# Turning v, p and three quarters of x2 with VectorE's block transpose through DRAM instead of TensorE, in a hybrid RWKV-7 and pooling trunk

## The chip, the cores and the metric

The kernel runs on one core of a Trainium2 chip. The metric is device time in microseconds (us) of the whole program, a median over several runs; a profiled execution has a time of its own, which is always told apart from the median here. The engines are named as in the profile: PE is TensorE's matmul, PEld its weight load, DVE is VectorE, ACT is ScalarE, POOL is GpSimd, SP is the sync engine, which here only issues DMAs. SPq and ACTq are the DMA issues of SP and of ACT.

## The reference

One layer of a decoder trunk on `x` of 512 positions by 2048 features, all float32: an input projection, 16 RWKV-7 heads of 64 beside a pooling branch, an output projection with a residual, and a gated embedding.

```python
h = rms_norm(x, norm_g)
z = h @ w_in                       # r, k, v, decay and rate inputs | gate | pool input | pool gate
zs = zs + (token_shift(zs) - zs) * mu
decay = exp(-exp(-softplus(-(w0 + tanh(wd) @ w_up)) - 0.5))
a = sigmoid(a0 + ad @ a_up)
kk = (k * k_k).reshape(B, T, N_HEADS, HEAD_SIZE)
kk = kk / maximum(norm(kk, axis=-1, keepdims=True), KK_EPS)
k = k * (1 + (a - 1) * k_a)
# per head and position: S = S (diag(w) - kk^T (a kk)) + v^T k;  y = S r
y = head_group_norm(wkv7_scan(r, decay, k, v, kk, a), ln_w, ln_b)
y_rwkv = (y + sum(r * k * r_k) * v) * silu(gate)
y_pool = per_group_matmul(windowed_mean(u) - u, w_pool) * pool_scale * silu(pool_gate)
x = x + concat(y_rwkv, y_pool) @ w_out
gate = sigmoid(x @ w_pg + b_pg)
x = x + gate * (p @ w_ple)
return rms_norm(x, final_g)
```

## The kernel before

Each large matrix product is made of three products of 128x128 by 128x512 blocks: an operand is split into a high part, which is a rounded copy (`whi`, `hhi`, `yhi`, `x2hi`: an ACT cast), and the rest (`wlo` and so on: a DVE subtraction). `wsplit` (L126 to L134) does that for a weight block: a DMA on SP into `raw`, the ACT cast at L132, the DVE subtraction at L133. The pools `raw`, `whi` and `wlo` hold four blocks each.

The program has three stretches. **The first** (to 715 us) makes h, transposes it, and then runs the input projection as a stream of matmuls: `pump(n)` (L492) puts the next n steps of that stream (the column groups z of k, r, v and the gate of each pair of heads, and the pooling units `zb`, `pp` and `pple`) into PE's program between the small matmuls of the recurrence, so that PE's order is fixed and the recurrence's waits are covered by the stream. The recurrence goes through eight groups j, each of two heads. For each of them:

- `prepare(j)` makes from k, r, v the scaled operands `ar` (L594, L597), `bk` (L596), `kp`, and stores `bk` to DRAM (`bkd`), from where it is read back turned in blocks of 32 by 32 (`bg`, L662).
- `invert(j)` is a substitution of 31 steps of two small DVE operations (L674, L678) on `xw`, with the rows `n` that were stored to `nd` and loaded back spread over the partitions. Its steps are interleaved with the eight chunks of `recur(j-1)`: `step` lets HN = 2 of them follow each hop after the HS-th, ordered behind the DVE product `zs` of that hop. Its result goes to DRAM (`xd`) and back into `x1`, by four stores and four loads on SP.
- `gather(j)` computes decay and rate of group j+1 (`pu`, `pa` with the small weights `ur`, `ar` and their splits `us`, `as`, L526), turns v (`pv`, four transposes on PE, with two ACT copies at L707 and L708 into `uv`), sums the squares of k per head for group j+1 (`pss`, two matmuls in `norm_key`), turns `x1` (`y1`, two DVE transposes of 32x256 at L732), and then runs the small matmuls `pq`, `pmv` and `px` that finish the inverse.
- the key norm of group j+1 is `max(pss, 1e-24)` (L568) and a reciprocal of the full 128x512 tile (L572) on DVE, in `scale_key`.
- `recur(j)` runs eight chunks, each with PE products `py`, `pu`, `ps`, DVE products `zs` and `sbd`, and ACT copies `uv`. At its end the group's y is normalised (`st`, `mvr`, `rs`, `nt`, `ysb`: L862 to L873), gated (`yo`) and stored to `yd`.

**The second** (715.6 to 895.5 us) multiplies by w_out in `proj`: four groups `ec` of 512 columns, each with 16 steps of k, each step with four accumulators of three matmuls (`acc_o`). After a group `ec` the result is added to x (L1026), stored (`x2d`), and turned for the next stretch: 16 PE transposes (`px`, L1033) with four ACT casts into `x2hi` and four DVE subtractions into `x2lo`.

**The third** (to the end) multiplies by w_pg in the same way (`acc_g`), with the x2 just turned as the moving operand, gates the embedding and normalises.

What sets the order: PE's by the program text with `pump`; on DVE and ACT a scheduler places each instruction by priority and readiness, and `tc.issue_after(a)` forbids an instruction to stand ahead of `a` on its engine; SP issues its DMAs one after another in its own order, and waits where a DMA's source isn't ready or its target isn't free.

## Time and profile before

| | before |
|---|---|
| median of 3 runs | 1085.27 us (1084.38 to 1087.19) |
| profiled execution, time | 1082.7 us |
| its span | 1081.0 us |
| PE busy | 1056.6 us (98%), 5996 instructions |
| DVE busy | 714.0 us (66%), 1851 instructions |
| ACT busy | 441.5 us (41%), 901 instructions |
| granted PE clock | 0.998 of full speed |

The span runs from the first to the last instruction; the profiled execution's time is 1.7 us longer. Busy time of PE counts a matmul from its start to its modelled end, and neighbouring matmuls overlap; what a matmul takes of PE's time is therefore read from the distance between the starts of two matmuls, not from its own duration. The instruction counts are those of the profile.

### The profile page before, as it was taken

To read this page: it belongs to the slowest core of one execution; us is meant where nothing else is said; L and a number is where in the kernel's file an instruction comes from. 1 tells how busy PE (TensorE), PEld (TensorE's weight loads), DVE (VectorE), ACT (ScalarE), POOL (GpSimd) and SP (SyncE) were. 2 spreads that over 40 slices of the span, in tenths; PEclk is the share of its full clock that TensorE was granted. 3 is DMA by queue.
4 is the path that set the end of the run, shared out by engine and by line. 5 is a ranking of instruction groups with operands and counts; after the bars stand their busy time and mean duration, and the time that the engine had idled before them with its cause. 6 is when DMAs were issued, how large, how long until landed. Compare 5 with 4: busy or idle time off the path is not lost.

```text
span 1081.0 us, 17106 instructions
## 1 busy us (share of the span) xinstructions
PE 1056.6 (98%) x5996; PEld 872.1 (81%) x5996; DVE 714.0 (66%) x1851; ACT 441.5 (41%) x901; POOL 75.0 (7%) x180
## 2 busy tenths in 40 slices
PE   5999999999999999999999999999999999999996
PEld 4888878888888887878788788888888888888885
DVE  6676978888779789787887857563432424445356
ACT  7633435335335354353352344553222222333337
POOL 2100010110110100200101201000000000000000
PEclk9999999999999999999999999999999999999999
DMA  7434443342634533434435343774434428355434
GB/s 236 117 115 111 139 116 88 116 120 74 168 88 114 144 89 105 120 89 112 106 91 158 100 129 111 239 243 141 171 121 143 166 98 271 122 182 161 169 98 156
DMA packets 212916, 146.94 MB, mean 136 GB/s; under 512 B 68085, under 2 KB 173150, under 8 KB 212830
## 3 DMA queue, kind: packets, MB, share of 16 engines
q1 hardware_dynamic: 192126, 112.28, 35.9%
q10 hardware_dynamic: 20704, 33.56, 9.4%
q8 instruction: 47, 0.77, 0.3%
q14 instruction: 39, 0.32, 0.1%
HBM read 122.21 MB, written 23.07 MB: 134 GB/s over the span
## 4 chain that ended last, share of the span: by engine, by line
PE 91%; DVE 4%; DMA 3%; ACT 2%; issue 1%; ACTq 0%; SPq 0%; DVEq 0%
PE acc_o L157 16%; PE acc_g L157 16%; PE zb L157 14%; PE zv L157 8%; PE zg L157 8%; PE zr L157 8%; PE zk L157 7%; PE py L157 2%; PE pu L157 2%; PE pple L157 2%; PE pm L157 1%; DMA n<-nd 1%; PE pp L157 1%; PE ps L157 1%; DMA xt<-in_x_dram 1%; PE pmv L157 1%
## 5 line engine op out<-in xcount | busy, mean ns | idle before, releaser
L133 DVE TENSOR_TENSOR wlo_g<-raw_g,whi_g 128x512 fp32r<-128x512 f32 x84 | 57.0, 685 | 74.4 <-ACT whi_g L132 72.3
L157 PE MATMUL zb<-hhi,whi_b 128*128 128x512 f32 x256 | 106.0, 414 | 0.0
L133 DVE TENSOR_TENSOR wlo_o<-raw_o,whi_o 128x512 fp32r<-128x512 f32 x64 | 43.9, 690 | 90.9 <-ACT whi_o L132 90.8
L157 PE MATMUL zb<-hhi,wlo_b 128*128 128x512 f32 x256 | 100.4, 392 | 0.0
L157 PE MATMUL acc_o<-whi_o,ylo 128*128 128x512 f32 x256 | 100.2, 391 | 0.0
L157 PE MATMUL acc_o<-whi_o,yhi 128*128 128x512 f32 x256 | 99.9, 390 | 0.0
L157 PE MATMUL zb<-hlo,whi_b 128*128 128x512 f32 x256 | 99.8, 390 | 0.0
L157 PE MATMUL acc_o<-wlo_o,yhi 128*128 128x512 f32 x256 | 99.7, 389 | 0.0
L132 ACT CAST whi_g<-raw_g 128x512 fp32r<-128x512 f32 x84 | 52.0, 621 | 105.3 <-PE acc_g L157 58.9
L157 PE MATMUL acc_g<-whi_g,x2hi 128*128 128x512 f32 x208 | 81.2, 391 | 0.0
L832 POOL TENSOR_SCALAR s0p<-sbd,pw 64x64 f32<-64x64 f32 x96 | 58.0, 604 | 332.0 <-DVE sbd L825 243.5
L157 PE MATMUL acc_g<-wlo_g,x2hi 128*128 128x512 f32 x208 | 80.9, 389 | 0.0
L157 PE MATMUL acc_g<-whi_g,x2lo 128*128 128x512 f32 x208 | 80.6, 389 | 0.0
L132 ACT CAST whi_o<-raw_o 128x512 fp32r<-128x512 f32 x64 | 39.9, 623 | 96.3 <-PE acc_o L157 96.3
L132 ACT CAST whi_b<-raw_b 128x512 fp32r<-128x512 f32 x64 | 39.7, 621 | 86.7 <-PE zb L157 29.2
L133 DVE TENSOR_TENSOR wlo_b<-raw_b,whi_b 128x512 fp32r<-128x512 f32 x64 | 43.6, 683 | 27.3 <-ACT whi_b L132 27.1
L157 PEld LDWEIGHTS zb<-hhi,wlo_b 128*128 128x128 f32 x256 | 48.0, 188 | 10.9
L678 DVE TENSOR_TENSOR xw<-xw,tm 128x60 f32<-128x60 f32 (+24 forms) x248 | 52.1, 210 | 7.0
L157 PEld LDWEIGHTS acc_o<-wlo_o,yhi 128*128 128x128 f32 x256 | 48.1, 188 | 9.9
L157 PEld LDWEIGHTS acc_o<-whi_o,ylo 128*128 128x128 f32 x256 | 48.1, 188 | 9.8
L157 PEld LDWEIGHTS acc_o<-whi_o,yhi 128*128 128x128 f32 x256 | 48.1, 188 | 9.7
L157 PEld LDWEIGHTS zb<-hhi,whi_b 128*128 128x128 f32 x256 | 48.2, 188 | 8.3
(283 smaller groups left out, 2529.6 us busy)
## 6 DMA issues: line engine op xcount, KB each, us to landing
raw_b<-in_w_in_dram SPq DMA_DIRECT2D x64, 256.0 KB
raw_o<-in_w_out_dram SPq DMA_DIRECT2D x64, 256.0 KB
raw_g<-in_w_pg_dram SPq DMA_DIRECT2D x64, 256.0 KB
raw_k<-in_w_in_dram SPq DMA_DIRECT2D x32, 256.0 KB
raw_r<-in_w_in_dram SPq DMA_DIRECT2D x32, 256.0 KB
raw_v<-in_w_in_dram SPq DMA_DIRECT2D x32, 256.0 KB
raw_g<-in_w_in_dram SPq DMA_DIRECT2D x32, 256.0 KB
bkd<-bk SPq DMA_DIRECT2D x8, 512.0 KB
```

Of the source, the lines that this page charges most:

```text
L132: nc.scalar.copy(hi, raw)
L133: nc.vector.tensor_tensor(lo, raw, hi.bitcast(F32), ALU.subtract)
L157: i = nc.tensor.matmul(*a, **k)
L678: nc.vector.tensor_tensor(xw[:, 0:n_, s + 1:32], xw[:, 0:n_, s + 1:32], tm[:, 0:n_, 0:w_], ALU.add)
L832: nc.gpsimd.tensor_scalar(s0p[hc, :], nxt[hc, hc], pcn[hc], None, ALU.mult)
```

## The change

1. **x2.** `x2d` is laid out by blocks, and for the first three groups `ec` the 16 PE transposes are replaced: during the next group, from step 5 on, SP issues up to three gathers per step (16 in all, `x2g`, each 32 partitions by 16 blocks by 32 elements), and in steps 8, 9, 11 and 12 one DVE transpose each of 128x512 makes `x2t`, which is split as before. The fourth group's turn stays on PE and moves ahead of a step's matmuls.
2. **v.** For the groups after the first, v is stored to `vd`, gathered back by four DMAs of SP (`vg`), and turned by two DVE transposes of 64x512 straight into `uv`. The four PE transposes and the two ACT copies of each such group go.
3. **p.** Eight gathers on SP read p by blocks, and two DVE transposes take the place of eight PE transposes.
4. **Key norm.** For groups 2 to 7 the squares' sum is copied by ACT, two of its rows are stored to DRAM, loaded as 128x8, clamped and inverted by DVE at that size, stored, and loaded twice with a broadcast to 64 partitions, all by SP. Squaring and summing move from `gather` into chunks 4 and 5 of the recurrence of two groups before.
5. **Substitution.** It starts one hop later (HS from 5 to 6) and does one more step at hop 21.
6. **Small weights and stores.** `ur` and `ar` (32 loads) are issued by SP, after the loads of `n`, instead of ACT; their ACT copies are ordered behind a copy of chunk 6 of the recurrence before. Seven stores of `yo` and six of `sgp` move from ACT's queue to SP's.

```diff
     def load_ab(j):
...
-                nc.scalar.dma_start(out=raw[64 * h:64 * h + 64, :], in_=src[0, :, jc])
+                nc.sync.dma_start(out=raw[64 * h:64 * h + 64, :], in_=src[0, :, jc])
...
             if kind == "p":
-                    pt = psM.tile([P, T], F32, name=f"ppt{k}", tag="m")
-                    for tt in range(NT):
-                        tr(pt[:, tt * P:(tt + 1) * P], pn[0][:, tt, k * P:(k + 1) * P], ident)
+                    pt = rw.tile([P, T], F32, name=f"ppt{k}", tag=("kk", "kp")[k])
+                    nc.vector.transpose(pt.rearrange("p (b k) -> p b k", k=32), pn[0][:, k])
...
     def norm_key(j):
...
-        late[0] = nc.vector.tensor_scalar(kk, ps, 1e-24, None, ALU.max)
+        if j < 2:
+            late[0] = nc.vector.tensor_scalar(kk, ps, 1e-24, None, ALU.max)
+            return
+        nc.scalar.copy(kk, ps)
+        nrd = dram.tile([2, T], F32, name=f"nrd{j}", tag="nrd")
+        nc.sync.dma_start(out=nrd, in_=kk[0::64, :])
+        nr = rw.tile([P, 8], F32, name=f"nr{j}", tag="nr")
+        nc.sync.dma_start(out=nr, in_=nrd.rearrange("h (p e) -> (h p) e", e=8))
+        nrs[j] = nr
+
+    def spread_norm(j):
+        nr, kk = nrs.pop(j), kks[j][0]
+        nc.vector.tensor_scalar(nr, nr, 1e-24, None, ALU.max)
+        nc.vector.reciprocal(nr, nr)
+        ird = dram.tile([2, T], F32, name=f"ird{j}", tag="ird")
+        nc.sync.dma_start(out=ird.rearrange("h (p e) -> (h p) e", e=8), in_=nr)
+        for h in range(2):
+            nc.sync.dma_start(out=kk[64 * h:64 * h + 64], in_=ird[h:h + 1].to_broadcast([64, T]))
 
     def scale_key(j):
-        nc.vector.reciprocal(kk, kk)
+        if j < 2:
+            nc.vector.reciprocal(kk, kk)
...
     def prepare(j):
+        if j:
+            vd = dram.tile([P, T], F32, name=f"vd{j}", tag="vd")
+            with tc.issue_after(read[-1].ins):
+                nc.sync.dma_start(out=vd, in_=v_)
+            vgs[j] = rw.tile([P, NT, 4, 32], F32, name=f"vg{j}", tag="t", bufs=4), vd
...
     def scores(j):
+        if j:
+            vg, vd = vgs[j]
+            with tc.issue_after(n_.ins):
+                for q in range(4):
+                    nc.sync.dma_start(out=vg[32 * q:32 * q + 32],
+                                      in_=vd.rearrange("(b k) (c q i) -> q k c b i", b=4, q=4, i=32)[q])
...
     def gather(j):
-            prepare_key(j + 1)
+            if j == 0:
+                prepare_key(1)
...
-        ps = psY.tile([P, T], F32, name=f"pv{j}", tag="y")
-        for tt in range(NT):
-            tr(ps[:, tt * P:(tt + 1) * P], v_[:, tt * P:(tt + 1) * P], ident)
-        pv = ps.rearrange("p (t c) -> p t c", c=P)
-        nc.scalar.copy(uv[0:64, 0::2, :], pv[0:64])
-        nc.scalar.copy(uv[64:128, 1::2, :], pv[64:128])
+        if j:
+            vg, _ = vgs.pop(j)
+            for h in range(2):
+                hr = slice(64 * h, 64 * h + 64)
+                nc.vector.transpose(uv[hr, h::2, :].rearrange("p c (b k) -> p c b k", k=32), vg[hr])
+        else:
...
         with tc.issue_after(yt[0].ins), tc.issue_after(yt[1].ins):
-            end = normed.pop()() if normed else yt[1]
-        if j + 1 < NJ:
-            with tc.issue_after(yt[0].ins), tc.issue_after(end.ins):
+            if normed:
+                normed.pop()()
+            if j + 1 < NJ:
                 scale_key(j + 1)
...
-                    for _ in range(HN):
+                    for _ in range(HN + (hop[0] == HE1)):
                         next(work, None)
...
+            if j + 2 < NJ and ch == 5:
+                norm_key(j + 2)
...
+            if j + 2 < NJ and ch == 4:
+                prepare_key(j + 2)
...
-    HS, HN = 5, 2
+    HS, HN, HE1 = 6, 2, 21
...
-    x2d = dram.tile([T, D], F32, name="x2d", bufs=1)
+    x2d = dram.tile([D // EC, EC // P, T, P], F32, name="x2d", bufs=1)
...
+    RD0, RDN, TURNS = 5, 3, (8, 9, 11, 12)
...
-            nc.scalar.dma_start(out=x2d[rows, es], in_=t_)
+            nc.scalar.dma_start(out=x2d[ec, :, rows, :].rearrange("c t e -> t c e"),
+                                in_=t_.rearrange("p (c e) -> p c e", e=P))
...
+        def turner(blocks, turned, ec=ec):
+            parts = [(c, q) for c in range(EC // P) for q in range(4)]
+
+            def side(i):
+                with tc.issue_after(wmade[0].ins), tc.issue_after(wmade[1].ins), tc.issue_after(wmade[2].ins):
+                    if i >= RD0:
+                        for c, q in parts[:RDN]:
+                            nc.sync.dma_start(out=blocks[32 * q:32 * q + 32, c],
+                                              in_=x2d[ec, c].rearrange("(b k) (q i) -> q k b i", k=32, i=32)[q])
+                        del parts[:RDN]
+                    if i in TURNS:
+                        c = TURNS.index(i)
+                        t_ = turned(c)
+                        nc.vector.transpose(t_.rearrange("p (b k) -> p b k", k=32), blocks[:, c])
+                        split(x2hi[:, 4 * ec + c, :], x2lo[:, 4 * ec + c, :], t_)
...
         if ec < D // EC - 1:
-            turn()
+            side = turner(...)
```

**DVE, before `pq` of group 3.** These are DVE's last twelve instructions up to the second transpose of `x1` into `y1` (`y_...<-x_...`, on which `pq` waits), before the change. `sig`, `kp` and `tha` belong to the decay, key and rate of group 4, `ve`, `rs` and `nt` to the norm of group 2's y.

```order
L591 TENSOR_SCALAR kp_4535<-tha_4311,dprm 128x512
L133 TENSOR_TENSOR wlo_wp_0_2314<-raw_wp_0_2311,whi_wp_0_2313 128x256
L150 TENSOR_TENSOR nt_4272<-nt_4272,rs_4269 128x8
L592 TENSOR_TENSOR kp_4535<-kp_4535,sk_3911 128x512
L151 SCALAR_TENSOR_TENSOR rs_4269<-nt_4272,rs_4269 128x8
L593 TENSOR_SCALAR tha_4311<-tha_4311 128x512
L149 TENSOR_TENSOR nt_4272<-rs_4269,ve_4270 128x8
L568 TENSOR_SCALAR kk_4284<-pss_4342 128x512
L150 TENSOR_TENSOR nt_4272<-nt_4272,rs_4269 128x8
L732 STREAM_TRANSPOSE y_4397<-x_4167 32x256
L151 SCALAR_TENSOR_TENSOR rs_4269<-nt_4272,rs_4269 128x8
L732 STREAM_TRANSPOSE y_4397<-x_4167 32x256
```

And the same place after the change, again the last twelve up to the second transpose.

```order
L615 TENSOR_TENSOR ar_4558<-sr_4101,pw_4340 128x4x2x64
L153 TENSOR_TENSOR nt_4315<-nt_4315,rs_4312 128x8
L133 TENSOR_TENSOR wlo_g_0_2321<-raw_g_0_2318,whi_g_0_2320 128x512
L154 SCALAR_TENSOR_TENSOR rs_4312<-nt_4315,rs_4312 128x8
L777 STREAM_TRANSPOSE y_4431<-x_4234 32x256
L152 TENSOR_TENSOR nt_4315<-rs_4312,ve_4313 128x8
L617 TENSOR_TENSOR bk_4559<-kp_4560,ipw_4341 128x4x2x64
L153 TENSOR_TENSOR nt_4315<-nt_4315,rs_4312 128x8
L618 SCALAR_TENSOR_TENSOR ar_4558<-sk_3936,dprm,pw_4340 128x4x128
L133 TENSOR_TENSOR wlo_g_1_2418<-raw_g_1_2415,whi_g_1_2417 128x512
L154 SCALAR_TENSOR_TENSOR rs_4312<-nt_4315,rs_4312 128x8
L777 STREAM_TRANSPOSE y_4431<-x_4234 32x256
```

The clamp of the key norm (L568) is gone from this place; both products into `ar`, that into `bk` and two weight splits `wlo_g` now stand ahead of the second transpose.

**SP, in the w_out stretch.** Before, the loads of w_out's blocks (`raw_o`) follow each other across the end of a group `ec`.

```order
L129 DMA raw_o_14_8374<-in_w_out_dram 128x512
L129 DMA raw_o_15_8392<-in_w_out_dram 128x512
L129 DMA raw_o_8_8458<-in_w_out_dram 128x512
L129 DMA raw_o_9_8476<-in_w_out_dram 128x512
L129 DMA raw_o_10_8494<-in_w_out_dram 128x512
```

After it, the gathers of the group `ec` that has just ended stand between the loads of the next one (its blocks come in the order 8 to 13, 0 to 7, 14, 15, so `raw_o_1` is the eighth).

```order
L129 DMA raw_o_0_8610<-in_w_out_dram 128x512
L129 DMA raw_o_1_8631<-in_w_out_dram 128x512
L1094 DMA x2g_8494<-x2d 32x16x32 x9
L129 DMA raw_o_2_8652<-in_w_out_dram 128x512
L1094 DMA x2g_8494<-x2d 32x16x32 x3
L129 DMA raw_o_3_8677<-in_w_out_dram 128x512
L1094 DMA x2g_8494<-x2d 32x16x32 x3
L129 DMA raw_o_4_8702<-in_w_out_dram 128x512
L1094 DMA x2g_8494<-x2d 32x16x32
L129 DMA raw_o_5_8721<-in_w_out_dram 128x512
```

Nine gathers now stand between the eighth and the ninth load, and seven more up to the twelfth.

**PE, at the turn of v in group 3.** Before, `pu` and `pa` (the last of `pa` stands first here) are followed by the four transposes and the stream, and the squares' sum `pss` comes three steps later.

```order
L157 MATMUL pa_4308<-lal,uaz_571 128x512
L161 MATMUL pv_4314<-ident,sv_3355 128x128 x4
L157 MATMUL zb_4229<-hhi,whi_b_0_2224 128x512
L157 MATMUL zb_4229<-hlo,whi_b_0_2224 128x512
L157 MATMUL zb_4229<-hhi,wlo_b_0_2225 128x512
L157 MATMUL zb_4229<-hhi,whi_b_1_2230 128x512
L157 MATMUL zb_4229<-hlo,whi_b_1_2230 128x512
L157 MATMUL zb_4229<-hhi,wlo_b_1_2231 128x512
L157 MATMUL zb_4229<-hhi,whi_b_1_2230 128x512
L157 MATMUL zb_4229<-hlo,whi_b_1_2230 128x512
L157 MATMUL zb_4229<-hhi,wlo_b_1_2231 128x512
L157 MATMUL pss_4342<-kqh_4286,blk 128x512
```

After it the stream follows `pa` at once.

```order
L160 MATMUL pa_4345<-lal,uaz_571 128x512
L160 MATMUL zb_4272<-hhi,whi_b_0_2232 128x512
L160 MATMUL zb_4272<-hlo,whi_b_0_2232 128x512
L160 MATMUL zb_4272<-hhi,wlo_b_0_2233 128x512
L160 MATMUL zb_4272<-hhi,whi_b_1_2238 128x512
L160 MATMUL zb_4272<-hlo,whi_b_1_2238 128x512
L160 MATMUL zb_4272<-hhi,wlo_b_1_2239 128x512
```

Between `pa` and `pq` PE has six matmuls fewer. Over the program PE has 84 fewer: the transposes `pv` go from 32 to 4, `px` of x2 from 64 to 16, and those of p from 8 to none.

More of the change, by code (lines that the diff above doesn't have):

```diff
@@ L513, in need @@
         return zt[nm, j]
-    pws, kks, late = {}, {}, [None]
+    pws, kks, nrs, vgs, read, late = {}, {}, {}, {}, [], [None]
     H1, H2, H3, H4, H5, HE = 6, 12, 20, 8, 13, 40
+    tail = []
     def decay_and_rate(j):
@@ L523, in decay_and_rate @@
                                     (ar_, as_, uaz[1], slice(0, 64), slice(64, 128))):
-            nc.scalar.copy(st, raw)
-            nc.scalar.copy(z_[hi, :], raw[hi, :])
+            with tc.issue_after(tail[0].ins) if tail else ExitStack():
+                nc.scalar.copy(st, raw)
+                nc.scalar.copy(z_[hi, :], raw[hi, :])
             nc.vector.tensor_tensor(st[lo, :], raw[lo, :], st[lo, :].bitcast(F32), ALU.subtract)
@@ L716, in gather @@
         d.update(uv=uv)
-        if j + 1 < NJ:
-            norm_key(j + 1)
+        if j == 0:
+            norm_key(1)
+        if 0 < j < NJ - 1:
+            with tc.issue_after(read[-1].ins):
+                spread_norm(j + 1)
         pump(H5)
@@ L892, in gate_out @@
                 nc.vector.tensor_tensor(yo, yo, sg, ALU.mult)
-                nc.scalar.dma_start(out=yd[j], in_=yo)
+                (nc.sync if j + 1 < NJ else nc.scalar).dma_start(out=yd[j], in_=yo)
             return gate_out
@@ L997, in proj @@
                     continue
-            for tt in tts if keep is None or i >= LATE else tts[:-1]:
-                ts_ = slice(tt * P, (tt + 1) * P)
-                first = i == (LATE if keep is not None and tt == NT - 1 else 0)
-                e_ = mm3(acc[tt], hi_[:, k, ts_], lo_[:, k, ts_], wh[:, 0, :], wl[:, 0, :], first, i == KT - 1)
             if aside is not None and i == 2:
@@ L1006, in proj @@
                     recall(0, lp)
-        return acc
+            if side is not None:
+                side(i)
+            for tt in tts if keep is None or i >= LATE else tts[:-1]:
+                ts_ = slice(tt * P, (tt + 1) * P)
+                first = i == (LATE if keep is not None and tt == NT - 1 else 0)
+                e_ = mm3(acc[tt], hi_[:, k, ts_], lo_[:, k, ts_], wh[:, 0, :], wl[:, 0, :], first, i == KT - 1)
+        return acc
+    RD0, RDN, TURNS = 5, 3, (8, 9, 11, 12)
+    side = None
     ples = {}
@@ L1019, in trunk_kernel @@
         es = slice(ec * EC, (ec + 1) * EC)
-        acc = proj(w_out, yhi, ylo, ec, "o", order)
+        acc = proj(w_out, yhi, ylo, ec, "o", order, side=side)
         x2 = []
```

46 lines of the change are left out of this document (31 added, 15 removed).

## The prediction

> **What bounds the kernel now.** I read the page's busy line and chain first, then the stretches, then what PE waited for.
>
> ```profile
> span 1081.0 us, 17106 instructions
> PE 1056.6 (98%) x5996; PEld 872.1 (81%) x5996; DVE 714.0 (66%) x1851; ACT 441.5 (41%) x901; POOL 75.0 (7%) x180
> PE 91%; DVE 4%; DMA 3%; ACT 2%; issue 1%; ACTq 0%; SPq 0%; DVEq 0%
> ```
>
> PE is busy 98% of the span and carries 91% of the chain that ends last. The table by stretch (two parts of the recurrence, w_out; busy time of PE, PEld, DVE, ACT, POOL, then clock, DMA share, GB/s) says that this holds everywhere, and that DVE is the next engine only in the recurrence.
>
> ```profile
> 45.00:330.00 285.00, 284.56 (x1743) 234.38 (x1742) 227.28 (x637) 119.81 (x252) 25.22 (x45) 1.00 0.43 115
> 330.00:640.00 310.00, 306.37 (x2053) 251.05 (x2053) 251.88 (x754) 127.94 (x277) 34.08 (x58) 1.00 0.42 111
> 715.60:895.50 179.90, 179.90 (x818) 148.87 (x817) 68.30 (x104) 52.39 (x88) 0.00 (x0) 1.00 0.43 147
> ```
>
> PE's waits from 45 us on are few; these are the ones inside the recurrence (total, times, longest):
>
> ```profile
> PE py L157 <- DVE sbd L825: 1.4, 2, 0.9
> PE pu L157 <- DVE zs L799: 1.0, 2, 0.6
> PE pbo L157 <- DVE kpl L138: 0.3, 1, 0.3
> ```
>
> So the time is the sum of PE's program plus about 3 us of stalls. Work taken from PE is won in full, unless what replaces it makes PE wait at a place where it now doesn't. The sum is made for PE: removed matmuls, stalls that go, stalls that come.
>
> **x2: 48 transposes off PE.** The chain through w_out, first group and last end:
>
> ```profile
> 715.63 43.52 PE acc_o L157 x192
> 759.15 1.06 PE px L1033 x9
> 895.49 4.53 PE acc_g L157 x20
> ```
>
> One matmul takes 43.52/192 = 0.2267 us; 768 of them are 174.1 us; the stretch lasts 895.49 - 715.63 = 179.86, so three turns cost 5.8 us. The timeline of one turn agrees: nine transposes take 759.98 - 758.99 = 0.99, three and four more 0.24 and 0.35, and after each break the next matmul is some 0.09 longer, 1.84 together.
>
> ```profile
> 758.99 1.23 PE L1033 MATMUL px<-ident,x 128*128 128x128 f32 x9
> 759.98 0.47 PE L157 MATMUL acc_o<-whi_o,yhi 128*128 128x512 f32 x1
> ```
>
> Three times 1.84 is 5.5, which I take: **-5.5 us** (at most -5.8).
>
> **v and p: 36 transposes off PE.**
>
> ```profile
> 327.78 0.60 PE L161 MATMUL pv<-ident,sv 128*128 128x128 f32 x4
> 328.45 0.39 PE L157 MATMUL zb<-hlo,whi_b 128*128 128x512 f32 x1
> 650.78 1.04 PE L161 MATMUL ppt<-ident,pn 128*128 128x128 f32 x8
> 651.66 0.39 PE L157 MATMUL py<-sbd,ar 128*128 128x128 f32 x2
> ```
>
> From the first `pv` to the second stream matmul behind it are 0.67 us, of which one matmul is 0.23: 0.44 per group, seven groups, **-3.1 us**. For p, 651.66 - 650.78: **-0.9 us**. The squares' sum `pss` only moves: nothing. PE's program is 9.5 us shorter.
>
> **What DVE gets.** Its price counts only where PE waits for it.
>
> ```profile
> L572 DVE RECIPROCAL kk<-kk 128x512 f32<-128x512 f32 x8 | 26.7, 3338 | 0.0
> 320.29 0.70 DVE L617 STREAM_TRANSPOSE bkn<-bg 128x512 f32<-128x512 f32 x1
> 320.92 0.13 DVE L678 TENSOR_TENSOR xw<-xw,tm 128x8 f32<-128x8 f32 x1
> 320.97 0.69 DVE L617 STREAM_TRANSPOSE bkn<-bg 128x512 f32<-128x512 f32 x1
> ```
>
> For groups 2 to 7 the reciprocal (3.34 us) and the clamp (0.69, row below) go, two small ones of 128x8 come (0.13 each, like the `xw` row); the two 64x512 transposes of v take 0.63 each, as a 128x512 one does to the start of what follows it (320.29 to 320.92). That is 3.34 + 0.69 - 0.26 - 1.26 = 2.5 us less per group, in a recurrence where DVE's products hold PE up now and then, as here:
>
> ```profile
> 429.90 0.49 PE L157 MATMUL pu<-zs,x 128*128 128x128 f32 x2 [0.61 <-DVE zs L799]
> ```
>
> I count this one and the `pbo` stall as gone: **-0.9 us** (bounds: none, and all 2.7 us of the three rows). The norm now comes by DRAM through two round trips. What needs it is `bk`, and behind that PE's `pm`:
>
> ```profile
> 345.73 0.68 DVE L600 TENSOR_TENSOR bk<-kk,ipw 128x512 f32<-128x512 f32 x1
> 350.70 2.06 PE L157 MATMUL pm<-ar,bk 64*128 64x128 f32 x32
> ```
>
> There are 4.3 us from the end of the one to the start of the other, and the reciprocal's 3.3 us ahead of it go: **0**. If the broadcast came later than that cover, each us beyond it would cost one in each of six groups.
>
> In w_out, DVE is busy 68 of 180 us and receives twelve transposes, 7.6 us: hidden. The substitution ends a hop later: its last `xw` operation, at 320.92 in group 3, goes to about 323, and two round trips of 2.9 us bring `x1` back by 329, before its turn at 332.76 (below): nothing. `ur` and `ar` are loaded behind `n`, most of a recurrence before `pu` needs them, and 14 ACT copies fewer matter nowhere with ACT at 41%: nothing.
>
> **What becomes late: `pq`.** PE's `pq` waits for the second DVE turn of `x1`. In group 3, before:
>
> ```profile
> 325.50 1.34 DVE L862 BATCH_NORM_STATS2 st<-ysb 128x6 f32<-128x64 f32 x8
> 327.30 0.66 DVE L138 TENSOR_TENSOR kql<-kk,kqh 128x512 fp32r<-128x512 f32 x1
> 332.09 0.69 DVE L568 TENSOR_SCALAR kk<-pss 128x512 f32<-128x512 f32 x1
> 333.27 0.43 DVE L732 STREAM_TRANSPOSE y<-x 32x256 f32<-32x256 f32 x1
> 333.82 0.69 DVE L133 TENSOR_TENSOR wlo_g<-raw_g,whi_g 128x512 fp32r<-128x512 f32 x1
> 334.50 0.69 DVE L594 TENSOR_TENSOR ar<-sr,pw 128x512 f32<-128x512 f32 x1
> 336.95 0.69 PE L157 MATMUL pq<-y,mt 32*32 32x32 f32 x32
> ```
>
> The turn ends at 333.70, 8.2 us after the statistics began; `pq` starts 11.45 us after them: 3.2 us of slack. In the new order, between the same two points, `kql`, `us` and the clamp go (0.6 + 0.3 + 0.6), and two transposes of v (1.26), two products into `ar` (0.60 and 0.65), `bk` (0.60) and two `wlo_g` (0.60 each, the distance from 333.82 to the small one behind it) come: 8.2 - 1.5 + 4.3 = 11.0 us. PE, without `pv` (0.44) and `pss` (0.45), comes to `pq` after 11.45 - 0.89 = 10.56. So it waits about 0.5, with the handover 0.7. The same count, with each group's own rows: 9.9 against 10.96 in group 1, 10.9 against 10.96 in 2, 11.5 against 10.95 in 4, 11.1 against 10.96 in 5, 10.2 against 12.3 in 6, 11.9 against 11.1 in 7, where two of the four reads of `x1` also stand behind a weight load on SP. The sum is 0.7 + 0.7 + 0.1 + 0.6 = **+2.1 us**. Below nothing is excluded, as PE has no stall at `pq` now; if each of seven counts is 0.5 short, it is +5.
>
> **SP in w_out.** This is the cover on which the largest term rests.
>
> ```profile
> 757.74 2.48 DVE L1026 TENSOR_TENSOR x<-acc_o,x 128x512 f32<-128x512 f32 x4
> 758.46 2.12 ACTq L1027 DMA_DIRECT2D x2d<-x  x4
> 627.73 1.00 SPq L689 DMA_DIRECT2D x<-xd  x2
> 630.63 0.43 DVE L732 STREAM_TRANSPOSE y<-x 32x256 f32<-32x256 f32 x1 [0.53 <-DMA x<-xd]
> L662 SPq DMA_DIRECT2D bg<-bkd x32: 568/617/3007, 85.0 to 593.5; - x32
> L132 ACT CAST whi_o<-raw_o 128x512 fp32r<-128x512 f32 x64 | 39.9, 623 | 96.3 <-PE acc_o L157 96.3
> ```
>
> The last store of a group's x2 is issued by 760.6 and lands, at the 2.9 us from a read's issue to its reader in the second pair of rows, by 763.4. Then nine gathers at 0.617 us each (median of the nearest kind, 32 partitions of 128 B runs) take SP to 769.0, and the ninth weight block lands and is split by 773.2 (2.9 + 0.62 + 0.69). PE needs it eight steps of 12 x 0.2267 after 758.99, at 780.8. ACT's idle time ahead of these casts, 96.3 us, ends with PE freeing a buffer and never with a load, so SP has this room, and the term is **0**.
>
> The Trainium skill, page "DMA: Bandwidth & Descriptors", section "Specifications", speaks against the gathers: it gives 512 B as the smallest transfer for full rate, with a read-modify-write below it. No run so far shows what 128 B runs do beside the weight loads of w_out; by that rule the gathers would lie nearer to the 3.0 us end of the row than to its median.
>
> **The sum.** -5.5 - 3.1 - 0.9 - 0.9 + 2.1 = -8.3 us. Span 1081.0 - 8.3 = 1072.7, profiled execution 1082.7 - 8.3 = 1074.4. The median stood 2.6 us above the profiled execution, so **1077.0 us** for the median. Its own range, from the bounds: -5.8 - 4.0 - 2.7 = -12.5 gives 1072.8; -9.5 + 5 = -4.5 gives 1080.8.
>
> **Rivals.**
>
> *The gain of the recurrence is eaten there.* SP gets 13 stores, 32 small loads and 28 gathers of v on top, and DVE's order decides PE's waits. If stalls at `pq`, or at `pu` for late small weights, take what v, p and the reciprocal give, only x2 is left: 1085.3 - 5.5 = 1079.8; if they take 3 us more, 1083. For it: the counts above are within 1 us of the limit in five of seven groups. Against: DVE has 2.5 us less to do per group.
>
> *The gathers starve w_out.* Nine gathers stand ahead of the ninth weight block. It must be issued by 780.8 - 4.2 = 776.6, so from 763.4 they have 13.2 us, 1.47 each. Beyond that PE waits three times. At 2.0 us each the loss is 3 x 4.8 = 14 us, the time 1077.0 + 14 = 1091, slower; at the row's longest, 3.0 us, it is 41 us, 1118. The gain is used up at 3 x 9 x (t - 1.47) = 8.3, t = 1.78. Against: the median 0.617, and a DMA share of 0.43. For: the longest of 32 did take 3.0.
>
> *The transposes are worth their busy time.*
>
> ```profile
> L1033 PE MATMUL px<-ident,x 128*128 128x128 f32 x64 | 9.1, 277 | 0.0
> ```
>
> 84 x 0.277 = 23.3 us instead of 9.5: 1077.0 - 13.8 = 1063. Against it stands the chain's 5.8 us for 48; the durations overlap.
>
> The Trainium skill, "TensorE: Matmul & The Clock Gate", section "Part 4: PE-mode transpose", gives about 275 ns for one in a kernel's context and so would put it there; the row's duration agrees with that figure, the distance of the starts (0.11 us) does not.
>
> *It moves nothing that sets the end.* Excluded for PE's program, which is 84 matmuls shorter; left for stalls that happen to make up 8 us.
>
> **Chances and range.** Forecast 0.60; recurrence eats its part 0.20 (two thirds of it still faster); gathers starve 0.08; busy time 0.06; something else at no change or slower 0.06. What can be told from no change is 0.3%, 3.3 us: faster below 1082.0, slower above 1088.5. Faster 0.60 + 0.13 + 0.06 = 0.79, same 0.07 + 0.04 = 0.11, slower 0.08 + 0.02 = 0.10. The range takes in the forecast's own and the first rival, without the tail beyond: 1072.5 to 1084.
>
> **What would show it.** w_out's stretch at 174 to 175 us with no idle time of PE, and DVE transposes between the weight splits: x2 right; PE waiting for `whi_o` or `wlo_o` at the ninth step: the gathers. PE waits named `pq` behind DVE `y`, 2 us in all, in groups 3, 4 and 7: the new stall right. No PE wait on `pu` behind `us`, nor on `pm` behind `bk`: the moved loads and the norm right. The forecast is wrong if PE's idle time from 45 us to the end exceeds before's by more than 5 us, or if the recurrence loses more at `py`, `pu`, `ps` than it did.

## The result and the profile after

The changed kernel takes 1075.1 us (median of 6 runs, 1073.26 to 1077.76); the kernel before, run beside it, 1084.97 us (6 runs, 1084.38 to 1087.19). The ratio is 0.9908, 95% interval 0.9891 to 0.9924: 9.9 us faster. The forecast was 1077.0, 8.3 us faster.

The two profiled executions lie off their medians by more than some terms of the forecast, and in opposite directions: the one of before, 1082.7 us, was faster than all of its timed runs, the one of after, 1077.76, is the slowest of its six. Between the traces there are therefore only 5 us. The page of after, in the lines that were shown of before (span, busy time, chain):

```profile
span 1076.0 us, 17131 instructions
PE 1047.7 (97%) x5912; PEld 864.6 (80%) x5912; DVE 711.7 (66%) x1879; ACT 435.0 (40%) x893; POOL 72.6 (7%) x180
PE 81%; DVE 9%; DMA 5%; ACT 2%; issue 2%; SPq 1%; ACTq 0%; DVEq 0%
```

PE has 84 instructions fewer and still bounds the kernel, but its share of the chain fell from 91% to 81%: more of the path goes by DVE and by DMAs. The chain through w_out, and PE's waits from the recurrence on (total, times, longest):

```profile
716.45 174.08 PE acc_o L160 x768
890.53 5.44 PE acc_g L160 x24
```

```profile
PE py L160 <- DVE sbd L874: 3.1, 4, 1.6
PE pq L160 <- DVE y L777: 2.0, 4, 0.7
PE pu L160 <- DVE zs L844: 1.4, 3, 0.8
PE pq L160 <- DVE sw L423: 0.4, 1, 0.4
PE pq L160 <- DVE nt L153: 0.4, 1, 0.4
```

The releaser that the profile names is the last DVE row to end: `sw` in group 5 and `nt` in group 2 are small rows that end just behind the turn `y`, which is what `pq` reads.

w_out is one unbroken run of 768 matmuls, 174.08 us: the 5.8 us of x2's transposes are won in full. In the recurrence this execution wins nothing: from the first `zk` to the first `acc_o` the timelines give 715.47 - 35.45 = 680.0 us before and 716.29 - 35.94 = 680.4 after. Most of the 4 us of `pv` and `ppt` that PE no longer does there went into waits, 3.8 us before and 7.3 after. Of these the `pq` waits were forecast; the `py` waits were not. The 3.8 us of before contain one wait of 1.1 us that the prediction's list leaves out, at `px` of group 5; it is gone after:

```profile
486.24 0.69 PE L157 MATMUL px<-x,q 32*32 32x32 f32 x32 [1.11 <-issue]
```

**The `pq` waits** stand where the prediction put them, here for groups 3 and 4:

```profile
341.75 0.69 PE L160 MATMUL pq<-y,mt 32*32 32x32 f32 x30 [0.73 <-DVE y L777]
415.87 0.69 PE L160 MATMUL pq<-y,mt 32*32 32x32 f32 x30 [0.65 <-DVE y L777]
```

**The `py` waits** come from a DMA. DVE's first step of the substitution waits for the rows `n`, which have been stored to DRAM and are read back; the `sbd` product that PE needs is queued behind it. Before, at group 3, and after, the read's issue on SP, DVE's first step, and after also PE's wait:

```profile
284.85 1.20 SPq L656 DMA_DIRECT2D n<-nd  x2
291.05 0.19 DVE L674 TENSOR_TENSOR tm<-i,n 128x31 f32<-128x31 f32 x1 [2.13 <-DMA n<-nd]
```

```profile
287.57 1.17 SPq L682 DMA_DIRECT2D n<-nd  x2
296.16 0.19 DVE L709 TENSOR_TENSOR tm<-i,n 128x31 f32<-128x31 f32 x1 [4.50 <-DMA n<-nd]
298.92 0.49 PE L160 MATMUL py<-sbd,ar 128*128 128x128 f32 x2 [1.60 <-DVE sbd L874]
```

From the end of the issue to the first step are 291.05 - 286.05 = 5.0 us before and 296.16 - 288.74 = 7.4 us after. Summed over the eight groups it is 41.6 us before and 50.9 after.

**SP in w_out** has less room than reckoned. After the first group `ec`, in the changed kernel: SP's issues, and the ACT cast of the ninth weight block, which now waits for its load.

```profile
765.10 7.56 SPq L1094 DMA_DIRECT2D x2g<-x2d  x9
773.06 0.35 SPq L129 DMA_DIRECT2D raw_o<-in_w_out_dram  x1
776.87 0.62 ACT L132 CAST whi_o<-raw_o 128x512 fp32r<-128x512 f32 x1 [5.36 <-DMA raw_o<-in_w_out_dram]
777.52 0.69 DVE L133 TENSOR_TENSOR wlo_o<-raw_o,whi_o 128x512 fp32r<-128x512 f32 x1 [5.29 <-ACT whi_o L132]
```

The gathers begin at 765.1 (forecast 763.4) and take 0.84 us each (forecast 0.617); the block is split at 778.2, and PE needs it at 716.45 + 24 x 2.72 = 781.7. 3.5 us of cover are left where 7.6 were reckoned. The share of the DMA engines (next to last column) is higher than in about the same stretch of before, which stands first:

```profile
761.00:769.00 8.00, 8.00 (x39) 6.60 (x38) 4.47 (x7) 3.65 (x7) 0.00 (x0) 1.00 0.64 224
```

```profile
761.60:770.00 8.40, 8.40 (x38) 6.94 (x37) 2.77 (x4) 2.48 (x4) 0.00 (x0) 1.00 1.00 268
```

Part of that is there ahead of the first gather: from 761 to 764 the share is 1.07 to 1.11 in each microsecond, under the stores of x2 and the loads of weights. A share of 1.00 is thus not a ceiling.

### The profile page after: what moved, and what is told of

It is laid out like the page before. It is cut to its first block, busy times and chain, and to the rows that moved or that the text cites. A ratio compares the mean times of both kernels' runs of the same rounds, so it can differ in the third digit from the quotient of the medians.

```text
span 1076.0 us, 17131 instructions
## 1 busy us (share of the span) xinstructions
PE 1047.7 (97%) x5912; PEld 864.6 (80%) x5912; DVE 711.7 (66%) x1879; ACT 435.0 (40%) x893; POOL 72.6 (7%) x180
## 4 chain that ended last, share of the span: by engine, by line
PE 81%; DVE 9%; DMA 5%; ACT 2%; issue 2%; SPq 1%; ACTq 0%; DVEq 0%
PE acc_o L160 16%; PE acc_g L160 16%; PE zb L160 10%; PE zv L160 7%; PE zr L160 7%; PE zg L160 6%; PE zk L160 6%; PE py L160 2%; PE pple L160 2%; DMA n<-nd 1%; PE pu L160 1%; PE pm L160 1%; DMA x<-xd 1%; PE pp L160 1%; PE ps L160 1%
## 5 line engine op out<-in xcount | busy, mean ns | idle before, releaser
L133 DVE TENSOR_TENSOR wlo_o<-raw_o,whi_o 128x512 fp32r<-128x512 f32 x64 | 43.9, 690 | 81.0 <-ACT whi_o L132 72.8
L160 PE MATMUL acc_o<-whi_o,yhi 128*128 128x512 f32 x256 | 94.7, 389 | 0.0
```

Source lines behind the costliest of these rows:

```text
L133: made.append(nc.vector.tensor_tensor(lo, raw, hi.bitcast(F32), ALU.subtract))
L160: i = nc.tensor.matmul(*a, **k)
```

## The experiments

Three questions were open: is x2's part worth exactly its PE time; are the `pq` waits a matter of DVE's order; and what makes the `py` waits, which move the time from run to run. Each group of four kernels (e1 to e4, e5 to e8, e9 to e12) ran on one chip beside runs of the kernel before, and is compared by the ratio to it. The second group had no run of the changed kernel beside it; but e6 and e7 differ from it only behind the recurrence, so that their stretch serves as its base there. "Stretch" below is the recurrence's, from the first `zk` to the first `acc_o` in the profiled execution; "landing" is the time from the end of `n`'s issue to DVE's first step, summed over eight groups. Waits at other places (`px`, `pss`, `pyt`) are told in the text.

| run | median us | ratio to before (95%) | stretch | waits at pq | waits at py, pu, pbo, ps | landing |
|---|---|---|---|---|---|---|
| before | 1084.97 | 1 | 680.0 | none | 2.7 | 41.6 |
| changed kernel | 1075.1 | 0.9908 (0.9891 to 0.9924) | 680.4 | 2.8 | 4.5 | 50.9 |
| e1, the same | 1074.61 | 0.9901 (0.9883 to 0.9919) | 678.7 | 2.3 | 4.5 | 49.6 |
| e2, x2 alone | 1081.0 | 0.9953 (0.994 to 0.9965) | 683.9 | none | 6.1 | 46.1 |
| e3, ur and ar by ACT | 1073.41 | 0.9885 (0.987 to 0.99) | 675.4 | 2.3 | 1.2 | 43.6 |
| e4, turn of x1 first | 1072.77 | 0.988 (0.9865 to 0.9895) | 673.3 | 0.5 | 1.1 | 45.0 |
| e5, start later | 1080.59 | 0.9965 (0.9952 to 0.9977) | 683.3 | 4.9 | 0.8 | (DVE comes later) |
| e6, gathers twice | 1102.76 | 1.0167 (1.0152 to 1.0182) | 676.2 | 2.3 | 1.9 | 46.5 |
| e7, fourth turn on DVE | 1079.77 | 0.9958 (0.9943 to 0.9973) | 676.2 | 2.9 | 1.7 | 45.5 |
| e8, norm on the full tile | 1080.57 | 0.9968 (0.9956 to 0.998) | 683.2 | 2.1 | 1.3 | 43.9 |
| e9, the same | 1073.25 | 0.9885 (0.9866 to 0.9904) | 676.0 | 3.0 | 1.2 | 45.6 |
| e10, v on PE | 1076.63 | 0.9916 (0.9896 to 0.9937) | 678.2 | none | 2.5 | 46.7 |
| e11, norm as before | 1075.76 | 0.991 (0.989 to 0.9929) | 677.7 | 2.6 | 2.2 | 44.5 |
| e12, e3 and e4 together | 1070.79 | 0.9857 (0.9836 to 0.9879) | 672.4 | 0.5 | 0.9 | 44.3 |

**e1 and e9, the changed kernel again.** No edit.

> The changed kernel again, as the base of the others and for a second trace of it. In the first trace PE idles in the recurrence at places of two kinds: at pq behind the turn y (2.8 us with what is counted beside it) and at py and pu behind DVE (4.5 us), the longest 1.60 at 298.9 us, behind a DVE that had waited 4.50 us for the rows n. Theory L (the rows n land at varying times and that moves the time from run to run): the pq stalls come again at the same groups within 0.3 us, the py and pu stalls come elsewhere or smaller, and the time is 1073 to 1077. Rival F (the stalls are fixed by the order of the instructions): both kinds come again at the same places, and the spread of the times is from elsewhere.

> The changed kernel once more, as the base of the three that run beside it. If the chip doesn't matter: ratio 0.989 to 0.992, pq waits of 0.7, 0.65 and 0.45 us in groups 3, 4 and 5 as in both traces before, and py waits that depend on how long n takes to land in this run (5.0 to 5.5 us: under 1 us of py waits; 6 to 7: 3 us).

The `pq` waits came again in groups 3, 4 and 5 at 0.74, 0.65 and 0.45 us in both runs: they are made by the order of the instructions. The `py` waits are another matter. By e1 alone rival F was not out: its longest, 1.47 us, stands in group 3 again, where the first trace had 1.60, and in sum it has 3.6 us against 3.1. But e9, where `n` landed 4 us sooner in sum, has 0.2, and in e6 and e7, whose recurrence is the same, there are 1.0 and 0.8.

Group by group the tie is tight. In groups 3, 5 and 7 of all kernels that start the substitution at HS 6, ten such waits are listed, from 0.19 us (landing 5.99, e6) to 1.60 us (landing 7.42, the first trace), and each is its group's landing less 5.76 to 5.82 us; with a landing under 5.95 us none is listed. (A wait of 0.2 us late in the stretch, the same in all these traces, is not among them; it is the whole of e9's 0.2.) Group 1 has waited 0.66 and 0.70 us at landings of 7.23 and 7.27; groups 2, 4 and 6 never. In the order of before, with HS 5, the same difference in groups 3, 5 and 7 is 5.0 us (0.52 at 5.52 before; 1.21 at 6.22 in e2). The later start of the substitution thus gave `n` 0.8 us more room, which the long landings of the first trace hid.

e2 shows the swing from the other side: its program in this stretch is that of the kernel before, and it took 683.9 us there against 680.0, with 3.4 us more waits and 4.5 us more landing. So the time that `n` takes differs between executions of the same instructions, and it moves the total by some 3 us. e1 and e9 ran on different chips; that the chip alone makes the difference is unlikely, as the five times of e1, on one chip, spread over 5.7 us. Theory L holds, with one correction: not the two kernels differ so much as the two executions that were profiled.

**e2, x2's part alone.** The kernel before with the third stretch's code and w_out's of the changed kernel.

```diff
-            turn()
+            side = turner(...)          # and x2d by blocks, as in the change; nothing else of it
```

> The kernel before with the first part of the change alone (x2's first three groups by gathers and DVE). Theory: the part is worth its PE time in full, 5.8 us by the trace of w_out (179.9 to 174.1), so 1085.0 - 5.8 = 1079.2, ratio 0.9947, and the w_out stretch is 174.1 us without a PE wait. Rival: part of the 9.9 us measured for the whole comes from something else in w_out or behind it, or the part costs something in the third stretch: then the time is off 1079.2 by more than 2 us.

1081.0 us, ratio 0.9953 (0.994 to 0.9965), 4.7 us by the medians, 3.8 to 6.5 by the interval; w_out is 174.08 us. The term of 5.5 to 5.8 us is inside the interval and exact in the trace. About half of the whole gain is x2's.

**e3, the small weights by ACT again.**

```diff
-                nc.sync.dma_start(out=raw[64 * h:64 * h + 64, :], in_=src[0, :, jc])
+                nc.scalar.dma_start(out=raw[64 * h:64 * h + 64, :], in_=src[0, :, jc])
     def prepare(j):
+        if j + 1 < NJ:
+            load_ab(j + 1)
     def scores(j):
-            with tc.issue_after(n_.ins):
-                load_ab(j + 1)
```

> The changed kernel with the loads of ur and ar again issued by ACT, early in the preparation of a group, instead of by SP right behind the loads of n. Theory L: those 32 loads, issued right behind n, are what makes n land 6 to 7.4 us after its issue instead of 5.0 to 5.3; without them DVE's wait for n falls back from 22.9 us in total to about 18, the py stalls behind it (1.60 and 0.70 us) go, and the time falls by 1 to 3 us (ratio 0.988 to 0.990). Rival: n lands late for another reason (the DMAs queued before it, the gathers of v); then DVE's wait stays above 21 us and the time within 1 us of the changed kernel's.

The `py` waits fell from 3.6 to 0.5 us, the landing from 49.6 to 43.6, and the four runs lie within 0.6 us. But the intervals of e3 and e1 overlap, and e4 and e9, which load `ur` and `ar` on SP as the change does, landed in 45.0 and 45.6. That the small loads cause the late landing is not shown; that a late landing causes the `py` waits is. w_out is 0.8 us longer here, 174.85 us, with a wait for `wlo_o` near its start.

**e4, the turn of x1 ahead.** `ar`, `bk` and the weight splits are ordered behind the second DVE turn.

```diff
+        hold[:] = yt[:1]                # the turn that comes second in DVE's order
...
+        with tc.issue_after(hold[0].ins) if hold else ExitStack():
             nc.vector.tensor_tensor(ar[...]...), (bk[...]...), (ar[...]...)
+        with tc.issue_after(hold[0].ins) if hold else ExitStack():
             made.append(nc.vector.tensor_tensor(lo, raw, hi.bitcast(F32), ALU.subtract))
```

> The changed kernel with the products into ar and bk and the weight splits that stand ahead of the second turn of x1 ordered behind it (about 2.4 us of DVE in group 3). Theory Q (pq waits because DVE's instructions ahead of the second turn take longer than PE needs to come there): the waits of pq behind y, 2.0 us of them, go to under 0.5, and the time falls by 1.5 to 2.5 us (ratio 0.9885 to 0.9895). Rival: the turn waits for its data (x1 read back from DRAM), so that pq stalls as before, or the stall comes back at pm or at the stream behind a late wlo_g: the time within 0.7 us of the changed kernel's.

PE's waits of this kind, in the changed kernel (e1) and in e4:

```profile
PE py L160 <- DVE sbd L874: 3.6, 4, 1.5
PE pq L160 <- DVE y L777: 1.9, 3, 0.7
PE pq L160 <- DVE sw L423: 0.4, 1, 0.4
```

```profile
PE pq L161 <- DVE y L779: 0.5, 1, 0.5
PE py L161 <- DVE sbd L877: 0.2, 1, 0.2
```

The `pq` waits are gone but for group 7's, where DVE stands idle 1.05 us because `x1` has not come back; the changed kernel's wait in group 7 is of that kind too (0.88 us of DVE's idle time in the first trace), and not one of order. Of the 1.8 us that left `pq`, 0.6 came back at `px` in group 5. The median is 1.8 us below that of e1, as theory Q had it, but the intervals overlap, so the traces carry the verdict rather than the times: against e9, whose `py` waits are as short, the stretch is 2.7 us shorter. `ar`, `bk` and the splits came late for nobody: no wait at `pm`.

**e5, the substitution one hop later.**

```diff
-    HS, HN, HE1 = 6, 2, 21
+    HS, HN, HE1 = 7, 2, (19, 20, 21)
```

> The changed kernel with the substitution beginning one hop later (HS 7) and an extra step at hops 19, 20 and 21, so that it ends in the same hop. Theory L, as it stands after the first runs (DVE comes to the substitution's first step before the rows n have landed, waits 15.8 to 22.9 us over eight groups, and the sbd products queued behind it make PE wait 0.3 to 3.6 us at py; how long n takes differs from run to run and not by who loads ur and ar): DVE's wait for n falls below 10 us, the waits at py below 0.5 us, the time by 1 to 3 us against the changed kernel's 1074.6 to 1075.1 (ratio 0.987 to 0.989), and the runs lie closer together than 1072.7 to 1078.4. Rival: the py stalls come from DVE's load in those hops and not from n; then they stay at 2 us or more, or pass to the hops with three steps, and the time is within 1 us of the changed kernel's or above.

1080.59 us, ratio 0.9965 (0.9952 to 0.9977): some 6 us slower than the changed kernel by the medians, and 7.1 us in the stretch against e6 and e7 on the same chip. The first half of theory L was right: DVE waits 3.7 us for `n` in place of 22.9, and PE 0.3 us at `py`. But `x1` comes back later: in group 7 DVE waits 1.89 us for it ahead of the second turn, the waits at `pq` are now 4.9 us, the longest 2.08, and 1.0 us of waits at `pss` are new. After the longest something else shows. Its row, and five single microseconds behind it (the third column from the end is the granted clock):

```profile
634.66 0.82 PE L160 MATMUL pq<-y,mt 32*32 32x32 f32 x30 [2.08 <-DVE y L777]
```

```profile
634.00:635.00 1.00, 0.34 (x20) 0.34 (x22) 0.82 (x4) 0.00 (x0) 0.00 (x0) 1.00 0.89 140
635.00:636.00 1.00, 1.00 (x32) 0.94 (x26) 1.00 (x6) 0.42 (x2) 0.00 (x0) 0.52 0.59 95
638.00:639.00 1.00, 1.00 (x18) 0.84 (x13) 0.00 (x0) 0.85 (x3) 0.00 (x0) 0.50 0.00 0
641.00:642.00 1.00, 1.00 (x4) 0.78 (x3) 0.53 (x1) 0.00 (x0) 0.00 (x0) 0.57 0.00 1
642.00:643.00 1.00, 1.00 (x7) 0.77 (x6) 0.27 (x1) 0.62 (x1) 0.00 (x0) 1.00 0.72 213
```

PE's clock is halved for 6.8 us, which costs 3.4 us on top of the wait. The hop of the start is thus a trade between two late DMAs, `n` at its beginning and `x1` at its end. HS 6 is the better of the two starts tried in this order; HS 5 was not tried in it.

**e6, each gather of x2 twice.**

```diff
-                        for c, q in parts[:RDN]:
+                        for c, q in [cq for cq in parts[:RDN] for _ in range(2)]:
```

> The changed kernel with each of the 48 gathers of x2 issued twice. It measures the cover that the prediction gave to SP in w_out. In the changed kernel the nine gathers take 7.56 us from 765.1 on (0.84 each), the ninth weight block is issued at 773.1, split by 778.2, and PE needs it at 781.7: 3.5 us of cover. With eighteen gathers it is issued some 7.6 us later: PE waits 4 us at the ninth step of three groups, and again at the tenth and eleventh, ahead of which six gathers take 3 to 5 us against a step of 2.72: 4 to 8 us per group, 12 to 24 in all, time 1087 to 1099, w_out 186 to 198 us. Rival (SP has the room that the prediction reckoned, 13.2 us for nine): the doubled gathers cost 15.1 us, 1.9 too many, so 3 x 2 = 6 us, time 1081.

1102.76 us, ratio 1.0167 (1.0152 to 1.0182), and w_out takes 201.9 us instead of 174.1. SP's issues after the first group, and what PE waits for:

```profile
761.22 14.49 SPq L1094 DMA_DIRECT2D x2g<-x2d  x18
775.81 0.43 SPq L129 DMA_DIRECT2D raw_o<-in_w_out_dram  x1
776.29 5.02 SPq L1094 DMA_DIRECT2D x2g<-x2d  x6
781.40 0.44 SPq L129 DMA_DIRECT2D raw_o<-in_w_out_dram  x1
781.89 5.18 SPq L1094 DMA_DIRECT2D x2g<-x2d  x6
```

```profile
780.43 0.50 PE L160 MATMUL acc_o<-whi_o,yhi 128*128 128x512 f32 x1 [2.60 <-ACT whi_o L132]
786.14 0.80 PE L160 MATMUL acc_o<-whi_o,yhi 128*128 128x512 f32 x1 [2.14 <-ACT whi_o L132]
791.86 0.50 PE L160 MATMUL acc_o<-whi_o,yhi 128*128 128x512 f32 x1 [1.03 <-ACT whi_o L132]
```

The doubled gathers cost more than either expectation. The ninth block stalls PE by 2.6 us; then the tenth and eleventh each have six gathers of 5 us ahead of them, longer than a step of 2.72 us, and stall it again; and the granted clock is 0.50 in the microseconds from 786 to 789 and 0.97 on average over the whole of w_out. The mechanism of the slower rival is real, and it was a factor of two in the number of gathers away.

**e7, the fourth turn on DVE too.**

```diff
-            acc = proj(w_pg, x2hi, x2lo, ec, "g", aside=turn if ec == 0 else None)
+            last = turner(<blocks in x3[3]>, <turned in x3[2]>, ec=LAST) if ec == 0 else None
+            acc = proj(w_pg, x2hi, x2lo, ec, "g", side=last, aside=(lambda: wmade[1]) if ec == 0 else None)
```

> The changed kernel with the fourth turn of x2 also by gathers and DVE, during the first sixteen steps of the third stretch, instead of the 16 transposes on PE. Theory (a turn on PE costs its distance in starts, 1.9 us as measured for the first three, 5.8 us together): 1.9 us less, ratio 0.988, no PE wait at acc_g in that stretch. Rival: in that stretch the loads of w_pg and of the embedding are as near to their limit as in w_out, and PE waits for whi_g or wlo_g: the time as the changed kernel's or above.

1079.77 us, ratio 0.9958 (0.9943 to 0.9973): slower than the changed kernel, as the rival had it. PE's longest wait is

```profile
PE acc_g L160 <- ACT whi_g L132: 5.1, 2, 4.2
```

with the 4.2 us at 909.68. Ahead of that weight block SP had issued six gathers in 10.50 us, beside the reads that the start of this stretch brings:

```profile
892.13 10.50 SPq L1094 DMA_DIRECT2D x<-x2d  x6
```

The clock was at half for 3.4 us behind the wait. From the first `acc_g` to the end this trace takes 191.9 us, those of e1 and e9 185.7: the same edit that is free in the middle of w_out costs 6.2 us at a place with less room, where the theory had 1.9 us less.

**e8 and e11, the key norm on the full tile again.** In e8 the clamp and the reciprocal are as before, in the place that the changed order gives them; e11 also puts the reciprocal behind the normalisation of y, as it was.

```diff
-        if j < 2:                        # both
-            nc.vector.reciprocal(kk, kk)
+        nc.vector.reciprocal(kk, kk)     # and no copy, no store, no spread_norm
...
-            if normed:                   # e11
-                normed.pop()()
-            if j + 1 < NJ:
+            end = normed.pop()() if normed else yt[1]
+        if j + 1 < NJ:
+            with tc.issue_after(yt[0].ins), tc.issue_after(end.ins):
                 scale_key(j + 1)
```

> The changed kernel with the key norm as before: the clamp and the reciprocal of the whole 128x512 tile on DVE, no spreading by DRAM (the squares' sum stays in the recurrence of two groups before). DVE gets 2.8 us more in each of six groups, SP five DMAs less. Theory S (the spread norm gives back stalls behind DVE): the time rises by the 0.9 us that the prediction gave it, at most 3 (ratio 0.991 to 0.993), and PE waits at pu or pbo near the place of the reciprocal as in the kernel before. Rival: DVE has room there and the spread norm's DMAs cost as much as it gives: within 0.7 us, or faster.

> The changed kernel with the key norm's clamp and reciprocal as before and also in the order of before: the reciprocal behind the normalisation of y (ysb), where the run with the full norm had it ahead in two groups. Theory S (that run lost 6 us because the 3.3 us of the reciprocal stood ahead of ysb: 2.6 us of waits at pyt and then PE at half clock for some 4 us): those waits go, and what is left is the price that the prediction gave, 1 to 2 us slower than the changed kernel (ratio 0.991 to 0.992). Rival: 2.8 us of DVE per group cost wherever they stand; then it stays 4 to 6 us slower (ratio 0.994 to 0.997).

e8 takes 1080.57 us (0.9968, 0.9956 to 0.998), e11 1075.76 us (0.991, 0.989 to 0.9929), the changed kernel beside e11 1073.25. In e8 two groups have the reciprocal ahead of `ysb`, and PE waits for `pyt` behind it, 1.41 and 1.15 us:

```profile
271.78 1.57 PE L164 MATMUL pyt<-ident,ysb 128*128 128x128 f32 x4 [1.15 <-DVE ysb L919]
```

```profile
273.00:274.00 1.00, 0.97 (x4) 0.83 (x5) 1.00 (x2) 0.60 (x1) 0.00 (x0) 0.85 0.00 0
274.00:275.00 1.00, 1.00 (x4) 0.78 (x3) 0.96 (x3) 0.18 (x1) 0.00 (x0) 0.50 0.00 0
277.00:278.00 1.00, 1.00 (x6) 0.80 (x5) 0.55 (x2) 0.76 (x3) 0.00 (x0) 0.94 0.31 85
```

In the order of before these waits go, and 2.5 us are left by the medians; the intervals of the ratios overlap, the times of the two kernels (1075.44 to 1077.76, and 1072.93 to 1074.48) do not. The trace has 1.7 us of it in the stretch, of which 0.8 are more waits at `pu` (1.8 against 0.9 in e9), and 0.8 us in w_out. The latter can't be laid to the norm, since e3 has the same 0.8 with the norm spread. The spread norm is worth some 1.7 to 2.5 us, and not the 6.

**e10, v on PE again.** `vd`, `vg` and the two DVE turns out, the four transposes and two ACT copies back for every group.

> The changed kernel with v turned again by four PE transposes and two ACT copies per group. Theory (the prediction's two terms): PE has 3.1 us more to do, DVE 1.26 us less ahead of each turn of x1, so that the waits at pq (2.3 to 2.8 us) nearly go: 0.3 to 1.0 us slower than the changed kernel. Rival 1 (the waits at pq stay, being due to ar, bk and the weight splits): 3 us slower. Rival 2 (the loads of v's blocks are what makes n land late): the DMAs of v gone, n lands in 5.0 to 5.5 us, the py waits go and the kernel is as fast as the changed one or faster by up to 1.5 us.

1076.63 us against 1073.25 beside it, 3.4 us slower; here too the ratios' intervals overlap, and the times (1075.03 to 1079.87, and 1072.93 to 1074.48) do not. It is the figure of rival 1 by the mechanism of the theory. Rival 2 is out: without the loads of v's blocks `n` landed in 46.7 us, against 45.6 with them. The waits at `pq` are all gone, 3.0 us of them. But 3.1 us of work came back, PE waits 1.3 us more at `py`, `pu` and `ps`, and another wait stands where group 5's `pq` wait was:

```profile
487.22 0.69 PE L160 MATMUL px<-x,q 32*32 32x32 f32 x32 [1.17 <-issue]
```

It is the one that the kernel before had at 486.24 (1.11 us). It stands behind `pq` in the same chain of small matmuls, and its size goes with what `pq` waited: none in the traces of the changed kernel, where `pq` of group 5 waits 0.45 us, 0.6 in e4 and e12, 1.1 to 1.2 in before, e2 and here, all without that wait. What holds `px` itself the profile does not name (`issue`). A stall taken away from a chain of small steps came back in part at its next step.

**e12, e3 and e4 together.**

> The changed kernel with both edits: the second turn of x1 ahead of ar, bk and the splits, and ur and ar loaded by ACT. If the two are worth 2 us each apart from each other: 4 us less than the changed kernel, ratio 0.986. If the second only matters through how n lands, and that is not of its making: the same as the first edit alone, ratio 0.988.

1070.79 us, ratio 0.9857 (0.9836 to 0.9879), the fastest kernel here: 2.5 us below the changed kernel beside it, 14.4 below the kernel before. The ratio is what was expected if the two parts add up, the 2.5 us are less than the 4 expected then. Whether e3's part adds to e4's is within the error.

## Why the prediction was right, point by point

**What bounds the kernel**: right. PE has 84 instructions fewer, w_out shows them in full, and in the recurrence the time moves with PE's waits.

**x2, -5.5 (at most -5.8)**: right at the upper figure; the difference of the stretches, 179.85 - 174.08 = 5.8, is the better way to read it than the sum of one turn's pieces. The rival by busy time (23.3 us for 84 transposes) falls with it: 48 of them took 5.8 us, not 13.3. So the figure of "TensorE: Matmul & The Clock Gate", "Part 4: PE-mode transpose", in the Trainium skill, about 275 ns in a kernel's context, doesn't give the gain here: the duration is such (277 ns), the distance is not (0.12 us each), and the distance is what PE pays.

**SP in w_out at nothing**: right in the result, wrong in the cover. Issue per gather was 0.84 us and not 0.617, the start 1.7 us later, the landing of the weight block 3.8 us and not 2.9: 3.5 us of cover in place of 7.6. What made the nine slow is open: they took 0.84 to 0.89 us each in all three groups, while the threes behind them took 0.5, so the size of their runs is not the whole of it, and in the first group the DMA engines' share was above 1.00 before the first of them started. The Trainium skill's rule on transfers under 512 B ("DMA: Bandwidth & Descriptors", "Specifications") was held against the gathers in the prediction; they stayed far from the 3.0 us end, and no run here separates the size of the runs from the traffic beside them. The price of the rival was mis-sized: by 3 x 9 x (t - 1.47), e6, where SP spends 14.49/9 = 1.61 us per gather that is needed, would lose 3.8 us; it lost 27.8 in w_out. The formula had left out the loads behind the ninth, and the clock; both are in e6's rows.

**v and p, -4.0**: right as PE's work. v's net worth is about 3.4 us by e10's median and 2.2 us by its stretch, more than the forecast's own terms would leave (3.1 less a good part of the `pq` waits): without v's turns on DVE, `px` waits 1.2 us where it did not, and `py`, `pu` and `ps` 1.3 us more. p alone was not tried.

**`pq`, +2.1**: right in place, and in size near enough (2.3 to 3.0 us in the traces). Forecast 0, 0.7, 0.7, 0.1, 0.6 for groups 2, 3, 4, 5, 7; measured 0.36, 0.73, 0.65, 0.45, 0.31 in the first trace, 2.8 with group 0's 0.32, which had not been counted. Counting DVE's rows between two marks, in the new order, was good to 0.4 us. But the terms were not all formed alike: with the 0.2 us of handover that group 3 got, group 5 would have been 0.3 and group 7 1.0. Group 5 measured 0.45; group 7 waits for `x1` to come back, not for DVE's rows, so that its 0.6 is near the measured 0.31 to 0.49 by luck. The prediction put the later way back of `x1` at nothing; in group 7 it costs that much.

**Recovered stalls, -0.9**: right for the two waits it named, `pu` at 429.90 and `pbo`: both are in the two traces of the order of before (before and e2) and in none of the changed kernel. What it missed is the 1.1 us at `px`, which are in both traces too and went as well, and the swing at `py`: it was taken from an execution in which `n` landed in 41.6 us and the `py` and `pu` waits were 2.4 us; e2, with the same program there, had 5.9.

**The sum**: closer than its parts. For the recurrence it had -4.0 - 0.9 + 2.1 = -2.8 us. Five traces of that stretch in the changed order (the first, e1, e6, e7, e9) lie between 676.0 and 680.4 us, 677.5 in the mean, the two of the order of before at 680.0 and 683.9, 682.0 in the mean: -4.5 us, which with the 5.8 of w_out comes near the 9.9 of the medians. In the mean the waits cancel, 5.5 us before and 5.4 after, where the forecast had 1.2 us more; two traces on one side make this a rough account. And one part was luck: the profiled execution was forecast at 1074.4 us and took 1077.76, and the 2.6 us that were added to come to the median had the wrong sign for the kernel after, whose profiled execution lies 2.7 above its median.

**Its own sign of being wrong** came true in one point: the recurrence was not to lose more at `py`, `pu` and `ps` than before's 2.4 us, and in the first trace and in e1 it lost 4.5. In e6, e7 and e9 it lost 1.9, 1.7 and 1.2. A sign taken from one execution of before, the one with the short landings, couldn't bear that weight. The other sign held: 3.5 us more idle time of PE, where 5 were allowed.

**The late landing of n**: not in the prediction, which moved 32 loads behind it on SP at no price. It costs up to 3 us in an execution where it is long. What makes it long is open: e3 leaves the small loads as a candidate, e4 and e9 show that it can be short with them, and e2 that it can be long without them.

## What to carry to other kernels

Price work taken from TensorE by the distance between the starts of matmuls, and what replaces it by counting rows in the new order from a mark that both orders share to the instruction that is waited for; x2 came within 0.3 us here, and each new wait within 0.4. Look for the DMA that the first instruction of an in-order sequence waits for: its landing varies from run to run, all that is queued behind it varies too, and a single trace may be 2 or 3 us to either side of the median. Measure how much later it may land before anything waits: here 5.0 us with one order and 5.8 with another, which says more than the sum of waits in one trace. A cover in a queue should be measured with what else is on the DMA engines at that moment, and the next few transfers in that queue belong to the price.
